# The last eight input blocks of a down-projection: from plain products to seven products per output pair

## The chip, the cores and the metric

The kernel runs on one core of one Trainium2 chip. The metric is the device time of one execution in microseconds (us), lower is better. [...]

## The reference

One layer of a decoder on 1024 tokens of width 1024, in float32: a norm, two attentions, gates, a residual, then a norm and a gated MLP of width 2816 with a short convolution, a residual, and a last norm. The part that matters here:

```python
def conv_ffn(xn, w_up, conv_w, conv_b, w_down):
    u = xn @ w_up
    ...
    gate, val = jnp.split(c, 2, axis=-1)
    return (jax.nn.silu(gate) * val) @ w_down      # (1024 x 2816) @ (2816 x 1024)

x = x + conv_ffn(xn, ...)
return rmsnorm(x, norm_final_w)
```

## The kernel before

All matrices are cut in blocks of 128 by 128; activations lie transposed, so that a tile holds 128 features by 1024 tokens, used as two halves of 512. TensorE multiplies in a reduced float format, so each float32 operand is split into a high part (a cast on ScalarE) and a low part (source minus high, on VectorE). A product of two blocks is then three matmuls: high by high, high by low, low by high. `split` and `parts_h` make the two parts of an activation, `load_w` and `split_pair` those of weights.

The down-projection (`down`) has 22 input blocks (the hidden tiles `hd`, which the earlier part stored in DRAM) and 8 output blocks, and it works in three stages.

*Blocks 0 to 5* are multiplied plainly, in 16 pieces (three blocks and one output each, both halves).

*Blocks 6 to 13* go by a seven-product scheme. The output pair m and m + 4, the two token halves, and two groups of four input blocks make a 2 by 2 by 2 product of large blocks. With A the weights (A11, A12 for output m; A21, A22 for m + 4) and B the activations, seven products of large blocks do in place of eight: A11 B11, A12 B21, S1 T1, S2 T2, S3 T3, S4 B22 and A22 T4. The S are sums of weight blocks, made on GpSimd by `sum_pair`; the T are differences of the activation blocks, made on VectorE by `sums_h`, once for all outputs. A product is 4 blocks by 3 matmuls. For each of the four pairs the kernel first makes A11 B11 (kept in a bank `y`) and A12 B21, and then, in a second loop over the pairs, the five others. Every product is added from its bank into `x3`, the residual stream, by VectorE.

*Blocks 14 to 21* are again multiplied plainly. Their activations come in by `load_h` in the second loop, four for each pair (`late`). Then follow, for each half of the tokens, all eight outputs, 24 matmuls each; the weights are loaded twice, once for each half. The last two outputs of the second half go in quarters of 256 tokens. `evac` adds the bank into `x3`, squares on ScalarE, adds the squares up, and multiplies by the last norm's weight.

`last_norm` gives the closing steps of a half or a quarter as a list: column sums of the squares on TensorE, the power on GpSimd, the spreading over partitions on TensorE, and the scales with their output transfers. These are taken out one by one between the products of later outputs.

Weights are fetched one step ahead: `next_w` takes the next entry of a queue and `ahead` prepares the one after it. The pool `wp` has three `raw` tiles for loads and two each of `wh` and `wl`; `uw` has two each of `sh` and `sl` for split sums; the sums themselves lie in two tiles `c`. Activation parts lie in 28 slots (`hp` with 19 and `hpb` with 9), used in turn; loads go through nine tiles `hr`. A scheduler orders each engine's instructions by the order in the code and by when it reckons their operands ready; at run time each engine keeps that order.

Of the kernel before, what the change touches and what calls it, by code (L numbers as in the profile page):

```python
# [17 lines left out]
P = 128  # L18
D = 1024
T = 1024  # L20
KC = D // P
# [8 lines left out]
DEFER = (4,8)  # L30
N1 = 6
LPAD, RPAD = 288, 480
HOLD = 1
# [10 lines left out]
class Trunk:  # L44
# [24 lines left out]
    def ahead(self, n):  # L69
        while len(self.wq) < n and self.wsrc and (self.wsrc[0][1] != "pair" or self.uw):  # L70
            src, nk, *eng = self.wsrc.pop(0)
            if nk == "sums":

                self.sums = self.split_pair(*self.sum_pair(src, True, "sl"), 1, 3)
            elif nk == "rest":
                self.sums["A22"] = self.load_w(src[1][:, 4:8], 4)
                self.wq.append(self.sums)
            elif nk == "pair":
# [28 lines left out]
    def split_pair(self, g, v, sa, sb, skip=0, end=4):  # L107
# [3 lines left out]
        for pool, h, l, src, names in ((self.wp, "wh", "wl", g, ("A11", "A12")), (self.uw, "sh", "sl", sa, ("S1", "S2")),  # L111
# [16 lines left out]
            for i, name in enumerate(names):  # L128
                ops[name] = hi[:, i], lo[:, i]
        self.pin, self.after = False, None  # L130
        return ops

# [73 lines left out]
    def run(self):  # L206
        nc, tc = self.nc, self.tc
        with ExitStack() as ctx:
# [20 lines left out]
            self.x2d = self.dp.tile([8, P, T], F32, name="x2d")  # L229
            self.hd = self.dp.tile([NF, P, T], F32, name="hd")  # L230
            self.yd = self.dp.tile([8, P, T], F32, name="yd")
            self.wp = ctx.enter_context(tc.tile_pool(name="wp", bufs=2))
# [14 lines left out]
    def plan(self):  # L247
# [20 lines left out]

        n, n2 = N1 // 2, NF - N1 - 8
        self.pieces = [(m, c) for m0 in (4, 0) for c in range(2) for m in range(m0, m0 + 4)]  # L270
# [600 lines left out]

    def product(self, ps, a, b, ks=range(4), first=True, last=True, skip=False, low_last=False):

# [3 lines left out]
        if low_last:  # L877
            for n, k in enumerate(ks):
                for i, x in enumerate(self.B[b, k]):
                    nc.tensor.matmul(ps, ah[:, k, :], x, start=first and n == i == 0, stop=False, skip_group_check=skip)  # L880
            for n, k in enumerate(ks):
                i = nc.tensor.matmul(ps, al[:, k, :], self.B[b, k][0], start=False, stop=last and n == len(ks) - 1, skip_group_check=skip)
            return i
        for n, k in enumerate(ks):
            bh, bl = self.B[b, k]
            nc.tensor.matmul(ps, ah[:, k, :], bh, start=first and n == 0, stop=False, skip_group_check=skip)  # L886
# [104 lines left out]
    def open_down(self):  # L991
        tc = self.tc
        self.dctx = ExitStack()
        self.hrp = self.dctx.enter_context(tc.tile_pool(name="hrp", bufs=HR, reuse_waits="tile"))
        self.hp = self.dctx.enter_context(tc.tile_pool(name="hp", bufs=HP, reuse_waits="tile"))
        self.nh = 0
# [5 lines left out]

    def parts_h(self, src):

        h = self.tl(self.hp if self.nh % (HP + HPB) < HP else self.hpb, [P, 2, H2], "h", F32R)
        self.nh += 1
        return self.split(h[:, 0], h[:, 1], src)
# [62 lines left out]
    def down(self):  # L1070

        nc, tc = self.nc, self.tc
        with ExitStack() as ctx:
# [3 lines left out]
            self.uw = e(tc.tile_pool(name="uwd", bufs=2, side="right", reuse_waits="tile"))  # L1077
            self.hpb = e(tc.tile_pool(name="hpb", bufs=HPB, side="right", reuse_waits="tile"))
            self.sfp = self.cpl, "c"
# [18 lines left out]
            def one(name, k, j, hf):  # L1098
                self.B[name, k] = self.parts_h(self.raw_h(N1 + j, hf))

            preps += [lambda k=k, n=n, o=o, hf=hf: one(n, k, k + o, hf) for n, o, hf in (("B11", 0, 0), ("B21", 4, 0), ("B22", 4, 1)) for k in range(4)]
            sums = [lambda k=k: self.sums_h(k) for k in range(4)]
# [37 lines left out]
            for m in range(4):  # L1140
# [30 lines left out]
            acc = self.tl(self.uw, [P, 2, H2], "sh")  # L1171
            js = range(N1 + 8, NF)
            q = H2 // 2

            def evac(ps, m, hf, a=0, b=H2):

                x = x3[:, m, hf * H2 + a:hf * H2 + b]
                tt(x, x, ps, ALU.add)
                sum_ = acc[:, hf, a:b]
                sq = sum_ if m == 0 else self.tl(self.uw, [P, b - a], "sl")  # L1180
                nc.scalar.activation(sq, x, AF.Square)
                if m and (m < KC - 1 or not hf):
                    tt(sum_, sum_, sq, ALU.add)
                nc.scalar.mul(x, x, self.vecs[:, C_NO + m:C_NO + m + 1])
                return sq

            tail = []
            for hf in range(2):
                for m in range(KC if hf == 0 else KC - 2):
                    w = self.next_w()  # L1190
                    ps = bank(m % 2)
                    mms(ps, w, hf, js)
                    evac(ps, m, hf)
                    for _ in range(1 if m < 4 else len(tail)):
                        if tail:
                            tail.pop(0)()
                if hf == 0:
                    tail = self.last_norm(psD, [acc[:, 0]], x3, 0, 0, H2, ((0, 2, nc.vector), (6, 8, nc.gpsimd), (2, 4, nc.vector), (4, 6, nc.vector)))

            ws = [(m, self.next_w()) for m in (KC - 2, KC - 1)]  # L1200
            for a, b in ((0, q), (q, H2)):
                for m, w in ws:
                    ps = bank(m % 2)[:, :q]
                    mms(ps, w, 1, js, a, b, lambda n, m=m: tail.pop(0)() if a and n == (4 if m < KC - 1 else 2) else None)
                    sq = evac(ps, m, 1, a, b)
                tail = self.last_norm(psD, [acc[:, 1, a:b], sq], x3, H2, a, b, ((0, 1, nc.vector), (1, 3, nc.vector), (6, 8, nc.gpsimd), (3, 6, nc.vector)) if a else
                                      ((0, 3, nc.gpsimd), (3, 5, nc.vector), (5, 8, nc.vector)))
# [98 lines left out]
```

## Time and profile before

| | |
|---|---|
| median of 3 runs | 1348.9 us (1347.94 to 1349.32) |
| the profiled execution | 1349.12 us |
| its span, first to last instruction | 1347.3 us |
| mean granted TensorE clock | 0.997 |
| five-product loop of blocks 6 to 13 | 1192.5 to 1246.9 us |
| last eight blocks | 1246.9 to 1337.8 us |
| closing norm and output after the last product | 1337.8 to 1347.3 us |

In the lines of windows, the first two numbers are the stretch and its length; then follow the busy time of PE, PEld (weight loads), DVE, ACT and POOL with the number of instructions in brackets, the granted clock, the share of the DMA engines and GB/s. In lists by time, a line has the start, the duration, engine, source line and operation, and in brackets how long the engine was idle before it and what released it.

### The profile page before, as it was taken

How to read it: one execution, taken by the hardware profiler on the slowest of the kernel's cores; microseconds unless marked ns; L12 is line 12 of the kernel's file. 1: busy time of each engine (PE TensorE's matmuls, PEld its weight loads, DVE VectorE, ACT ScalarE, POOL GpSimd, SP SyncE). 2: the span in 40 equal slices, each digit the busy share in tenths (PEclk: the TensorE clock that was granted, in tenths of full speed). 3: DMA queues.
4: the chain of work that ended last, by engine and by line, in shares of the span. 5: the costliest groups of instructions: out<-in, count | busy, mean ns of one | idle time of the engine just before them, and what ended most of it. 6: DMA issues, size and time to landing. Idle time of an engine off the chain costs nothing.

```text
span 1347.3 us, 17300 instructions
## 1 busy us (share of the span) xinstructions
PE 1328.9 (99%) x6304; PEld 1104.6 (82%) x6304; DVE 1036.0 (77%) x1557; ACT 616.1 (46%) x1003; POOL 470.6 (35%) x349
## 2 busy tenths in 40 slices
PE   7999999999999999999999999999999999999997
PEld 6888888888888777878888888888888888888887
DVE  7847775289899875465678999999999987986454
ACT  8432232276667665333454444444444434433343
POOL 0336552000102124641455555565555511231011
PEclk9999999999999999999999999999999999999998
DMA  6423443866553235334433222222222238552342
GB/s 257 146 105 150 148 156 141 251 175 188 141 149 130 87 114 207 129 110 155 141 107 96 79 79 94 78 94 74 83 94 74 86 136 315 197 180 67 94 138 81
DMA packets 62468, 179.48 MB, mean 133 GB/s; under 512 B 6832, under 2 KB 15152, under 8 KB 62384
## 3 DMA queue, kind: packets, MB, share of 16 engines
q1 hardware_dynamic: 50928, 160.98, 36.9%
q10 hardware_dynamic: 11456, 17.41, 3.5%
q8 instruction: 49, 0.80, 0.2%
q14 instruction: 35, 0.29, 0.1%
HBM read 129.61 MB, written 48.76 MB: 132 GB/s over the span
## 4 chain that ended last, share of the span: by engine, by line
PE 88%; POOL 4%; DVE 3%; DMA 3%; ACT 1%; issue 1%; POOLq 0%; SPq 0%; ACTq 0%; DVEq 0%
PE t L886 13%; PE t L887 13%; PE t L888 13%; PE y L1091 3%; PE d L1091 3%; PE t L880 3%; PE g L180 3%; PE sc L602 3%; PE g L181 3%; PE g L182 3%; PE y L1118 2%; PE d L1118 2%; DMA gr<-gd 2%; PE sc L182 2%; PE sc L181 2%; PE sc L180 2%
## 5 line engine op out<-in xcount | busy, mean ns | idle before, releaser
L1049 ACT ACTIVATE c<-us,vecs 128x512 f32<-128x512 f32 x80 | 61.3, 780 | 132.5 <-POOL us L1043 128.5
L1051 DVE SCALAR_TENSOR_TENSOR c<-us,vecs,c 128x512 f32<-128x512 f32 x160 | 110.4, 748 | 8.6 <-ACT c L1049 8.6
L145 ACT CAST wh<-raw 128x1024 fp32r<-128x1024 f32 (+2 forms) x60 | 60.8, 1013 | 107.6 <-PE sc L181 30.5
L1043 POOL TENSOR_TENSOR us<-us,rstd 128x1024 f32<-128x1024 f32 x38 | 99.6, 2641 | 4.5 <-DVE us L435 2.4
L147 DVE TENSOR_TENSOR wl<-raw,wh 128x1024 fp32r<-128x1024 f32 (+2 forms) x60 | 75.0, 1250 | 33.3 <-ACT wh L145 21.8
L123 DVE TENSOR_TENSOR sl<-sf,sh 128x1024 fp32r<-128x1024 f32 x62 | 87.5, 1413 | 11.5 <-ACT sh L122 11.5
L122 ACT CAST sh<-sf 128x1024 fp32r<-128x1024 f32 x62 | 63.4, 1048 | 60.4 <-PE t L887 44.2
L123 DVE TENSOR_TENSOR wl<-raw,wh 128x1024 fp32r<-128x1024 f32 (+1 forms) x35 | 74.2, 2120 | 3.7 <-ACT wh L122 3.6
L98 POOL TENSOR_TENSOR sf<-rv 128x512 f32<-128x512 f32 x30 | 41.2, 1375 | 100.6 <-DVE sl L123 57.9
L180 PE MATMUL g<-xh,wh 128*128 128x512 f32 x176 | 70.6, 401 | 0.1
L182 PE MATMUL g<-xh,wl 128*128 128x512 f32 x176 | 70.3, 400 | 0.0
L181 PE MATMUL g<-xl,wh 128*128 128x512 f32 x176 | 70.3, 399 | 0.0
L197 POOL TENSOR_TENSOR rs<-ms,mhalf 128x8 f32<-128x8 f32 (+2 forms) x9 | 14.5, 1607 | 157.7 <-DVE ms L195 147.1
L103 POOL TENSOR_TENSOR sf<-raw,rv 128x512 f32<-128x512 f32 x30 | 40.7, 1356 | 65.4 <-DVE sl L123 65.4
L606 DVE CUSTOM_DVE_ANT_0 L<-sc,bias 128x128 f32<-128x128 f32 (+7 forms) x64 | 47.7, 751 | 17.0 <-PE sc L602 13.9
L585 POOL MEMSET aT<- 128x128 f32 x32 | 6.1, 204 | 151.6 <-PE t L631 101.3
L607 ACT ACTIVATE L<-L,sm 128x128 f32<-128x128 f32 (+7 forms) x64 | 49.6, 778 | 20.0 <-DVE sm L606 17.3
L760 POOL TENSOR_TENSOR gr<-gr,rstd 128x1024 f32<-128x1024 f32 x16 | 41.2, 2583 | 41.7 <-DMA gr<-gd 41.5
L123 DVE TENSOR_TENSOR wl<-rv,wh 128x512 fp32r<-128x512 f32 x30 | 49.3, 1642 | 3.5 <-ACT wh L122 3.5
L1053 ACT ACTIVATE c<-c 128x512 f32<-128x512 f32 x40 | 24.0, 600 | 60.8 <-DVE c L1051 60.8
L602 PE MATMUL sc<-u,u 128*128 128x512 f32 (+2 forms) x192 | 49.6, 358 | 0.0
L182 PE MATMUL sc<-mh,wl 128*128 128x512 f32 x126 | 49.1, 390 | 0.3 <-DVE wl L147 0.3
(515 smaller groups left out, 4334.7 us busy)
## 6 DMA issues: line engine op xcount, KB each, us to landing
u<-qd SPq DMA_DIRECT2D x72, 256.0 KB, 6.5
raw<-in_w_down SPq DMA_DIRECT2D x27, 512.0 KB, 3.6
raw<-in_w_in SPq DMA_DIRECT2D x25, 512.0 KB, 4.2
hr<-hd SPq DMA_DIRECT2D x50, 256.0 KB, 5.4
raw<-in_w_up SPq DMA_DIRECT2D x23, 512.0 KB, 3.5
hd<-c SPq DMA_DIRECT2D x22, 512.0 KB, 2.6
rv<-in_w_up SPq DMA_DIRECT2D x21, 512.0 KB, 3.5
gr<-gd SPq DMA_DIRECT2D x16, 512.0 KB, 3.6
```

Of the source, the lines that this page charges most:

```text
L123: j = nc.vector.tensor_tensor(lo, src, hi.bitcast(F32), ALU.subtract)
L147: self.lo = (eng or nc.vector).tensor_tensor(wl, raw, wh.bitcast(F32), ALU.subtract)
L180: nc.tensor.matmul(ps, wh[:, kc + o, :], ah, start=first and n == 0, stop=False)
L181: nc.tensor.matmul(ps, wh[:, kc + o, :], al, start=False, stop=False)
L182: nc.tensor.matmul(ps, wl[:, kc + o, :], ah, start=False, stop=last and n == len(kcs) - 1)
L602: nc.tensor.matmul(sc[:, lo + n0:lo + n1], qs, k[c][part][:, n0:n1], start=part == 0, stop=part == 1)
L886: nc.tensor.matmul(ps, ah[:, k, :], bh, start=first and n == 0, stop=False, skip_group_check=skip)
L887: nc.tensor.matmul(ps, ah[:, k, :], bl, start=False, stop=False, skip_group_check=skip)
L888: i = nc.tensor.matmul(ps, al[:, k, :], bh, start=False, stop=last and n == len(ks) - 1, skip_group_check=skip)
L1043: (nc.vector if j == 0 else nc.gpsimd).tensor_tensor(u[:, 2:], u[:, 2:], self.rstd, ALU.mult)
L1051: nc.vector.scalar_tensor_tensor(c, u[:, o + k:o + k + H2], col(m, k), c, ALU.mult, ALU.add)
L1091: nc.tensor.matmul(ps, v[:, n, :], x, start=n == i == 0, stop=n == len(js) - 1 and i == 2)
```

## The change

The last eight blocks use seven products too. Even and odd blocks (14, 16, 18, 20 and 15, 17, 19, 21) form the two groups. `second_pair` loads a pair's two weight tiles, makes four sums on GpSimd, splits A11, A12, S2, S3 and A22 and stores the sums S1 and S4 in DRAM (`sd`). Five products of each pair run in a loop: A11 B11, A12 B21, the previous pair's S3 T3, A22 T4, S2 T2. The last two, S1 T1 and S4 B22, follow for all pairs at the end, in one bank one after the other, with their weights loaded from `sd`; pairs 2 and 3 do them in quarters. Weights are loaded once, and their sums written and read once more.

The activations come in twice. Eight raw loads (512 KB each) go into the slots that B11 and B21 of blocks 6 to 13 leave; there `diffs` makes the four differences in place, behind chosen adds of the pairs m = 0, 1 and 2. B11, B21 and B22 are loaded again through `hr`. Their splits go into named slots (`old` finds those of the former T tiles): B11, B21, T4, T2 and T3 are traced before the new loop (`prepare(24)`), T1 and B22 within it. The sums of squares lie in four `hr` tiles (`box`).

```diff
+    def second_pair(self, src, m):
...
+        tt(sa[:, 0], v[:, 0], v[:, 1], ALU.add)
+        tt(sb[:, 0], sa[:, 0], g[:, 0], ALU.subtract)
+        tt(sb[:, 1], g[:, 0], v[:, 0], ALU.subtract)
+        tt(sa[:, 1], g[:, 1], sb[:, 0], ALU.subtract)
+        nc.sync.dma_start(self.sd[m], sa.rearrange("p a k c -> p (a k) c"))
+        ops = {}
+        for pool, h, l, x, names in ((self.wp, "wh", "wl", g, ("A11", "A12")), (self.uw, "sh", "sl", sb, ("S2", "S3")), (self.wp, "wh", "wl", v[:, 1:2], ("A22",))):
...
-        src += [(self.w_dn[m, :, N1 + 8:, :], n2) for _ in range(2) for m in range(KC)]
+        src += [((self.w_dn[m, :, N2:, :], self.w_dn[m + 4, :, N2:, :]), "second", m) for m in range(4)]
+        src += [(self.sd[m], 8) if m < 2 else (self.sd[m], "idle") for m in range(4)]
...
-            late = [(hf, j) for hf in range(2) for j in range(N1 + 8, NF)]
+            old = lambda n, k: (base + 12 + 4 * k + "T1 T2 T3 T4".split().index(n)) % (HP + HPB)
...
+            def diffs(k, after):
+                b11, b12, b21, b22 = raws[k]
+                with tc.issue_after(after.ins):
+                    tt(b11, b12, b11, ALU.subtract)
+                    tt(b12, b22, b12, ALU.subtract)
+                    tt(b22, b22, b11, ALU.subtract)
+                    tt(b21, b22, b21, ALU.subtract)
...
+            more = [lambda k=k: read("B11", k, 0, 0, old("T1", k)) for k in range(4)]
+            more += [lambda k=k: read("B21", k, 1, 0, old("T2", k)) for k in range(4)]
+            more += [lambda k=k: ready("T4", k, base + 8 + k) for k in range(4)]
+            more += [lambda k=k: ready("T2", k, old("T4", k)) for k in range(4)]
+            more += [lambda k=k: ready("T3", k, old("T3", k)) for k in range(4)]
+            more += [lambda: box.append(self.tl(self.hrp, [P, H2], "hr")) for _ in range(4)]
+            more += [lambda k=k: ready("T1", k, base + 2 * k + 1) for k in range(4)]
+            more += [lambda k=k: read("B22", k, 1, 1, base + 2 * k) for k in range(4)]
...
+            for k in range(4):
+                load(k)
             for m, y in enumerate(ys):
...
-                tt(col(m + 4, 0), col(m + 4, 0), ps, ALU.subtract)
+                i = tt(col(m + 4, 0), col(m + 4, 0), ps, ALU.subtract)
+                if m in (1, 2):
+                    diffs(2 * m - 1, i)
                 self.product(y, w["S3"], "T3", first=False, skip=True)
                 for hf in range(2):
-                    tt(col(m + 4, hf), col(m + 4, hf), y, ALU.add)
-                for _ in range(4):
-                    hf, j = late.pop(0)
-                    self.load_h(j, hf)
...
+                    i = tt(col(m + 4, hf), col(m + 4, hf), y, ALU.add)
+                if m < 2:
+                    diffs(2 * m, i)
+            prepare(24)
...
+            def seventh(m):
+                self.product(ys[m], ws[m]["S3"], "2T3", first=False, skip=True)
+                evac(ys[m], m + 4, 0)
+                tt(col(m + 4, 1), col(m + 4, 1), ys[m], ALU.add)
+
+            for m in range(4):
+                w = self.next_w()
...
+                self.product(y, w["A11"], "2B11", skip=True, low_last=True)
+                tt(col(m, 0), col(m, 0), y, ALU.add)
+                self.product(ps, w["A12"], "2B21")
+                evac(ps, m, 0)
+                if m:
+                    seventh(m - 1)
+                ps = bank(0)
+                self.product(ps, w["A22"], "2T4")
+                tt(col(m + 4, 0), col(m + 4, 0), ps, ALU.subtract)
+                self.product(y, w["S2"], "2T2", first=False, skip=True)
+                tt(col(m, 1), col(m, 1), y, ALU.add)
+                prepare(4)
+            seventh(3)
...
+            def fifth(m, w, a=0, b=H2):
+                ps = bank(0)[:, :b - a]
+                self.product(ps, [x[:, 0:4] for x in w], "2T1", skip=True, cols=slice(a, b))
+                evac(ps, m + 4, 1, a, b)
+                return ps
+
+            def third(m, w, ps, a=0, b=H2, last=False):
+                self.product(ps, [x[:, 4:8] for x in w], "2B22", first=False, skip=True, cols=slice(a, b))
+                return evac(ps, m, 1, a, b, last)
```

More of the change, by code (lines that the diff above doesn't have):

```diff
@@ L31 @@
 N1 = 6
+N2 = N1 + 8
 LPAD, RPAD = 288, 480
@@ L870, in operands, with product @@
         tt(t4, t2, b21, ALU.subtract)
-    def product(self, ps, a, b, ks=range(4), first=True, last=True, skip=False, low_last=False):
+    def product(self, ps, a, b, ks=range(4), first=True, last=True, skip=False, low_last=False, cols=slice(0, H2)):
         nc = self.nc
@@ L879, in product @@
                 for i, x in enumerate(self.B[b, k]):
-                    nc.tensor.matmul(ps, ah[:, k, :], x, start=first and n == i == 0, stop=False, skip_group_check=skip)
+                    nc.tensor.matmul(ps, ah[:, k, :], x[:, cols], start=first and n == i == 0, stop=False, skip_group_check=skip)
             for n, k in enumerate(ks):
-                i = nc.tensor.matmul(ps, al[:, k, :], self.B[b, k][0], start=False, stop=last and n == len(ks) - 1, skip_group_check=skip)
+                i = nc.tensor.matmul(ps, al[:, k, :], self.B[b, k][0][:, cols], start=False, stop=last and n == len(ks) - 1, skip_group_check=skip)
             return i
         for n, k in enumerate(ks):
-            bh, bl = self.B[b, k]
+            bh, bl = (x[:, cols] for x in self.B[b, k])
             nc.tensor.matmul(ps, ah[:, k, :], bh, start=first and n == 0, stop=False, skip_group_check=skip)
@@ L1181, in evac @@
                 nc.scalar.activation(sq, x, AF.Square)
-                if m and (m < KC - 1 or not hf):
+                if hf in seen and not last:
                     tt(sum_, sum_, sq, ALU.add)
+                seen.append(hf)
                 nc.scalar.mul(x, x, self.vecs[:, C_NO + m:C_NO + m + 1])
                 return sq
[L1187 to L1198, printed above, removed]
@@ L1200, in down @@
-            ws = [(m, self.next_w()) for m in (KC - 2, KC - 1)]
-            for a, b in ((0, q), (q, H2)):
[L1202 to L1206, printed above, removed]
+            ys, ws = [], []
@@ new lines, in down @@
+            seventh(3)
+            assert not more
+            tail = self.last_norm(psD, [box[0]], x3, 0, 0, H2, ((0, 2, nc.vector), (6, 8, nc.gpsimd), (2, 4, nc.vector), (4, 6, nc.vector)))
+            def fifth(m, w, a=0, b=H2):
[6 more added lines that the diff above has]
+                return evac(ps, m, 1, a, b, last)
@@ new lines, in step @@
+            def step(n=1):
+                for _ in range(n):
+                    tail.pop(0)()
+            ws = [self.next_w() for _ in range(2)]
+            p = []
+            for m in range(2):
+                p.append(fifth(m, ws[m]))
+            step()
+            for m in range(2):
+                third(m, ws[m], p[m])
+                step()
+            ws += [self.next_w() for _ in range(2)]
+            for a, b in ((0, q), (q, H2)):
+                p = []
+                for m in (2, 3):
+                    p.append(fifth(m, ws[m], a, b))
+                    step()
+                sqs = [box[1][:, a:b], third(2, ws[2], p[0], a, b, True)]
+                if not a:
+                    step()
+                sqs.append(third(3, ws[3], p[1], a, b, True))
+                assert not tail
+                tail = self.last_norm(psD, sqs, x3, H2, a, b, ((0, 1, nc.vector), (1, 3, nc.vector), (6, 8, nc.gpsimd), (3, 6, nc.vector)) if a else
```

63 lines of the change are left out of this document (52 added, 11 removed).

## The prediction

> **What bounds the kernel now.** I read the page's busy line first, then the windows by stage, then the chain, and last VectorE's and GpSimd's own lists in time. The windows are cut at the stage borders: the MLP's hidden part, the four output pairs of the first seven-product part (m = 0 to 3), the start of the last eight blocks, the end.
>
> ```profile
> PE 1328.9 (99%) x6304; PEld 1104.6 (82%) x6304; DVE 1036.0 (77%) x1557; ACT 616.1 (46%) x1003; POOL 470.6 (35%) x349
> core 0: us, PE busy (x) PEld busy (x) DVE busy (x) ACT busy (x) POOL busy (x), PEclk, DMA share, GB/s
> 720.00:1100.00 380.00, 380.00 (x1678) 314.67 (x1677) 364.22 (x430) 166.00 (x227) 201.17 (x155) 1.00 0.25 84
> 1192.50:1206.10 13.60, 13.60 (x62) 11.26 (x61) 12.56 (x16) 3.24 (x6) 6.23 (x5) 1.00 0.65 210
> 1206.10:1219.70 13.60, 13.60 (x62) 11.26 (x61) 7.60 (x10) 2.74 (x4) 5.22 (x5) 1.00 0.25 80
> 1219.70:1233.30 13.60, 13.60 (x62) 11.26 (x61) 8.22 (x10) 3.16 (x4) 2.54 (x2) 1.00 0.26 79
> 1233.30:1246.90 13.60, 13.60 (x62) 11.26 (x61) 11.84 (x17) 6.85 (x10) 0.00 (x0) 1.00 0.14 39
> 1246.90:1268.70 21.80, 21.80 (x98) 18.06 (x97) 8.23 (x10) 7.11 (x10) 0.00 (x0) 1.00 0.33 98
> 1324.90:1337.80 12.90, 12.90 (x111) 12.90 (x109) 6.30 (x11) 5.34 (x10) 2.01 (x2) 1.00 0.03 10
> 1337.80:1347.30 9.50, 2.06 (x12) 1.49 (x11) 2.46 (x5) 1.30 (x3) 2.50 (x3) 0.61 0.59 208
> ```
>
> TensorE fills every stage of the down-projection at full clock; nothing holds it until 1337.8, and 9.5 us of closing norm and output follow. So a matmul taken out is worth its whole spacing as long as VectorE (DVE) keeps up. DVE has spare time there: 7.60 and 8.22 of 13.6 us busy in m = 1 and 2, 8.23 of 21.8 in the last part.
>
> ```profile
> 1246.94 5.44 PE d L1091 x24
> 1252.38 5.44 PE y L1091 x24
> 1319.53 5.44 PE y L1091 x24
> 1324.97 2.87 PE d L1091 x24
> ```
>
> In the chain, one output half of the last eight blocks is 24 matmuls in 5.44 us: 0.2267 us for one of 512 columns, and 2.87 / 24 = 0.120 for one of 256.
>
> **What goes.** Before, the last blocks take 16 output halves of 24 matmuls, 384 in units of 512 columns (the last two outputs' second halves run as quarters of 256). After, they take 4 pairs x 7 products x 12 = 336, with as many quarters as before (2 pairs x 2 products x 2 quarters x 12 = 96). So 48 go: 48 x 0.2267 = **10.88 us**. The 28 products of 2.72 us last 76.2 us instead of 87.1. [...]
>
> **What DVE gains.** Prices first; the lists give start, duration, engine, line.
>
> ```profile
> 1169.35 0.68 DVE L1018 TENSOR_TENSOR hr<-hr,hr 128x512 f32<-128x512 f32 x1
> 1169.95 0.68 DVE L1016 TENSOR_TENSOR hr<-hr,hr 128x512 f32<-128x512 f32 x1
> 1234.58 1.22 DVE L123 TENSOR_TENSOR sl<-c,sh 128x1024 fp32r<-128x1024 f32 x1
> 1235.71 0.68 DVE L800 TENSOR_TENSOR h<-hr,h 128x512 fp32r<-128x512 f32 x1
> ```
>
> Start to start, a 512-wide operation costs 0.60 us and a 1024-wide one 1.13. Added are 16 in-place differences (9.6 us), 12 more operand splits (28 for 16: 7.2) and 16 more PSUM adds into x3 (9.6); the weight splits stay about even: (1.13 + 1.13 + 0.60) x 4 and 4 x 1.13 make 16.0 us, against 16 x 1.13 = 18.1. That is some 24 us more DVE work in a stretch about 11 us shorter. Three places matter.
>
> *m = 1 and 2 of the first part.* The differences are put behind chosen adds there: two sets of four in m = 1 (one just past m = 0's last add), two around m = 2, 4.8 us each. DVE goes from 7.60 to 12.4 and from 8.22 to 13.0 of 13.6. Nothing is late by itself: the adds have four banks to hide in. Their eight raw loads (4 MB) wait on SP for B11's and B21's slots, which TensorE's first products release by 1192.5; the pair loads queue behind them. The DMA share is 0.65 and then 0.25, so they land within m = 0 and 1, before their differences. I put both at nothing; without that cover DVE would stand at a difference for about one landing, the 3.6 us of this row:
>
> ```profile
> raw<-in_w_down SPq DMA_DIRECT2D x27, 512.0 KB, 3.6
> ```
>
> *The entry to the new part.* New operands go into the slots of old ones, so they can be split only as the last pair (m = 3: five products of 12 x 0.2267 = 2.72 us from 1233.3) releases those: B11 into T1's at 1236.0, B21 into T2's at 1238.8, T4 into B22's at 1241.5, T2 into T4's at 1244.2, T3 into T3's at 1246.9. They are wanted at 1246.9, 1249.7, 1252.4, 1255.1, and for T3 at 1263.3. The product S2 T2 also accumulates into bank y, so it waits for the add that reads A11 B11 out of it, and that add was traced behind T3's splits. DVE's list from 1233.3 to that add: 10 adds (6.0), S34 of m = 3, A11 and S2/S3 of the new pair (3 x 1.13 = 3.4), its A22 (0.6), 20 splits (12.0): **22.0 us**, for 21.8 until S2 T2 is due at 1255.1. Undisturbed it just fits. It isn't undisturbed:
>
> ```profile
> 1189.58 1.30 POOL L98 TENSOR_TENSOR c<-raw 128x512 f32<-128x512 f32 x1 [24.83 <-DMA raw<-in_w_down]
> 1190.84 1.75 POOL L103 TENSOR_TENSOR c<-raw,raw 128x512 f32<-128x512 f32 x1
> 1192.56 1.74 POOL L102 TENSOR_TENSOR c<-c,raw 128x512 f32<-128x512 f32 x1
> 1194.37 1.62 POOL L104 TENSOR_TENSOR c<-raw,c 128x512 f32<-128x512 f32 x1
> 1191.36 0.68 DVE L1147 TENSOR_TENSOR x<-x,y 128x512 f32<-128x512 f32 x1
> 1191.95 4.59 DVE L800 TENSOR_TENSOR h<-hr,h 128x512 fp32r<-128x512 f32 x3
> 1222.27 1.29 POOL L103 TENSOR_TENSOR c<-raw,raw 128x512 f32<-128x512 f32 x1 [5.74 <-DVE sl L123]
> ```
>
> While GpSimd (POOL) forms a pair's weight sums, three splits took 4.59 us (1.53 each), while the add from PSUM kept its 0.68. Those three cost 4.59 - 1.80 = 2.8 us. POOL's own operation grew from 1.30 to about 1.7. The new pair 0's sums wait for the tile c that S34 of m = 3 gives back (1234.58 + 1.22 = 1235.8), as the last row's waited; pair 1's follow some 8 us later. So POOL runs through much of exactly this stretch, and it makes 0 to 2 x 2.8 = 5.6 us more. With pair 1's A11 split possibly ahead (1.13) and the differences of m = 1 and 2 slowed in the same way (POOL ran 5.22 and 2.54 us there; at 2.8 per 5.1 us that is 2.9 and 1.4, against room of 1.2 and 0.6, so 2.5 carried over), TensorE stands between 0 and 0.2 + 5.6 + 1.1 + 2.5 = 9.4 us. I take **4 us**: most of one pair's disturbance and part of the other's, as the splits are about half of DVE's list and the row's 2.8 is for splits alone. The next thing late would be pair 1's A11 remainder, which its product uses last and which has 1.8 us of cover.
>
> *The loop and the tail.* A pair from m = 1 on costs DVE 8 adds (4.8), 2.9 of weights, 2.4 of T1 or B22 splits and 2.8 of disturbance: 12.9 of 13.6 us. The bank y now has 8.2 us of cover instead of 5.4, so I count nothing; at the far end 1 us a pair. The stored sums (512 KB out and in for each pair) follow 13.6 us apart, and SP's next weight loads queue behind a store that waits for POOL; each landing is 3 to 4 us, hidden unless that store slips by more than 5. In the tail, bank d is shared by S1 T1 and S4 B22, so the second waits until the first is read: 2.72 us of cover in whole halves, 1.43 in quarters, where a scale of 1.21 us may be ahead on DVE.
>
> ```profile
> 1302.93 1.21 DVE L1238 TENSOR_TENSOR x<-x,d 128x1024 f32<-128x1024 f32 x1
> 1332.50 0.36 PE L188 MATMUL d<-ones,sl 128*128 128x1 f32 x2
> 1332.72 0.36 PE L188 MATMUL d<-ones,sh 128*128 128x1 f32 x2
> ```
>
> Each quarter's column sums read three tiles instead of two: 2 more matmuls of one column at 0.22 / 2 = 0.11 us, twice: 0.44, of which the last quarter hides one. I count **0.3 us**; the waits in the quarters are between 0 and 4 x 0.4 = 1.6, and I take 0, since the last adds are dropped there. The closing 9.5 us stay.
>
> **Sum.** The profiled execution took 1349.12 us with a span of 1347.3, 0.2 us above the median of the runs shown, 1348.9. 1349.1 - 10.9 + 0.3 + 4.0 = 1342.5, and against the median **1342.3 us**, 0.5% faster. About 0.2% (2.7 us) is what a measurement can tell from no change: 1346.2 to 1351.6.
>
> **The rivals.**
>
> *DVE keeps up.* For it: in the hidden part DVE is 364 of 380 us busy with POOL at 201, and TensorE never waits. Against it: there operands stand ready for the next block, here slots open one by one. No stall gives 1348.9 - 10.9 + 0.3 = 1338.3. Chance 0.20.
>
> *The gain is eaten.* Both disturbances in full, the carried lateness too, and the loop's 1 us: 8 to 11 us of stalls, 1346.3 to 1349.3. Chance 0.14.
>
> *Slower: entry splits one by one behind POOL.* DVE serves its list in order; if pair 0's and pair 1's sums run without a gap while the 16 splits of B11, B21, T4 and T2 are made, each costs 1.53 instead of 0.60, 14.9 us in all, with TensorE standing at each product for its own four. That gives 1348.9 - 10.9 + 0.3 + 14.9 = 1353.2; it decides from 13.3 us of stalls. For it: POOL's 1.7 us each when disturbed, eight sums, 13.7 us. Against it: that covers only about half of the stretch, and adds from PSUM pass undisturbed. Chance 0.14.
>
> *The clock falls in the stall.*
>
> ```profile
> 1338.00:1340.00 2.00, 0.83 (x6) 0.74 (x6) 0.41 (x2) 0.92 (x2) 0.47 (x2) 0.99 0.46 160
> 1340.00:1342.00 2.00, 1.12 (x4) 0.72 (x4) 0.66 (x2) 0.23 (x1) 0.56 (x1) 0.50 0.75 265
> ```
>
> Within the last 4 us, where TensorE is busy 1.95 of 4, the granted clock goes from 0.99 to 0.50. [...] Against it: the lateness shows as several waits (B21, T4, T2, y) with matmuls between. Chance 0.08.
>
> **How the numbers follow.** The forecast, 2 to 7 us of stalls (1340.3 to 1345.3), has 0.44. Faster by over 0.2%: 0.44 + 0.20 + 0.08 = 0.72; within: 0.14; slower: 0.14. The range runs from just under the forecast's end into the case of no stall, 1338.8 (which leaves its lower part out), to the end of the eaten gain, 1349.0; the slower case lies outside.
>
> **What would show it.** The page's TensorE count falls by 48 and rises by 4, to 6260. In the windows TensorE stays full up to about 1246.9; then the waits should list TensorE behind DVE's splits and the add on y within the first four products, some 4 us in all, with splits of about 1.5 us while POOL is busy and 0.68 otherwise. The loop from pair 1 on should hold 13.6 us per pair with DVE over 90%. I am wrong in kind if TensorE waits for a DMA or ScalarE there, if it loses several us per pair in the loop or in the quarters, or if the differences hold up m = 1 and 2.

## The result and the profile after

The changed kernel takes 1343.6 us (median of 7 executions, 1343.26 to 1346.88), the kernel before 1348.68 beside it (7 executions, 1347.94 to 1349.32): a ratio of 0.9968, 95% interval 0.9956 to 0.9979. Run again in a later comparison it took 1343.65 against 1348.13, 0.9965 (0.9953 to 0.9978). So it is faster by 0.3%, 4.5 to 5.1 us, where 10.9 us of matmuls were taken out and 6.6 us were forecast.

The busy line and windows of the kernel after, at the same stages as the prediction's (all stages come 2.3 us earlier, because an earlier part of this execution was shorter by that). PE is TensorE, DVE VectorE, ACT ScalarE, POOL GpSimd, SP the queue of SyncE that issues most of the transfers; PSUM are the accumulator banks.

```profile
PE 1321.7 (99%) x6264; PEld 1097.4 (82%) x6264; DVE 1065.8 (79%) x1603; ACT 621.7 (46%) x1019; POOL 495.6 (37%) x365
```

```profile
1203.80:1217.40 13.60, 13.60 (x62) 11.14 (x61) 13.42 (x16) 3.21 (x5) 6.67 (x5) 1.00 0.23 77
1217.40:1231.00 13.60, 13.53 (x60) 10.89 (x59) 13.46 (x19) 3.10 (x3) 5.00 (x3) 1.00 0.27 79
1231.00:1244.60 13.60, 13.60 (x62) 11.27 (x61) 13.60 (x20) 12.55 (x22) 5.78 (x4) 1.00 0.23 77
1244.60:1262.06 17.46, 15.14 (x58) 11.19 (x57) 17.46 (x23) 5.88 (x10) 5.67 (x4) 0.90 0.29 93
1262.06:1275.66 13.60, 13.60 (x61) 11.26 (x60) 11.62 (x16) 6.43 (x9) 7.80 (x4) 1.00 0.44 134
1275.66:1289.26 13.60, 13.60 (x61) 11.26 (x60) 11.93 (x14) 7.71 (x11) 6.33 (x4) 1.00 0.47 173
```

Before, VectorE had 7.60 and 8.22 of 13.6 us to do in m = 1 and 2. Now it is full from there to the end of the entry (13.42, 13.46, 13.60, 17.46 of 17.46), and the entry is the one stage in which TensorE stands: 2.3 of 17.46 us. From pair 1 on TensorE is full again. The granted clock of the entry, 0.90, is the second thing to see.

How TensorE's wait at the entry comes about is read from the list by time, GpSimd first, then VectorE, ScalarE and TensorE:

```profile
1243.94 1.30 POOL L148 TENSOR_TENSOR c<-raw 128x512 f32<-128x512 f32 x1 [4.83 <-DMA raw<-in_w_down]
1245.20 1.74 POOL L150 TENSOR_TENSOR c<-raw,raw 128x512 f32<-128x512 f32 x1
...
1244.32 1.47 DVE L158 TENSOR_TENSOR wl<-raw,wh 128x512 fp32r<-128x512 f32 x1
1245.71 3.47 DVE L832 TENSOR_TENSOR h<-hr,h 128x512 fp32r<-128x512 f32 x2
...
1250.30 7.30 DVE L832 TENSOR_TENSOR h<-h,h 128x512 fp32r<-128x512 f32 x12
1257.53 1.21 DVE L158 TENSOR_TENSOR wl<-raw,wh 128x1024 fp32r<-128x1024 f32 x1
...
1248.67 1.05 ACT L157 CAST sh<-c 128x1024 fp32r<-128x1024 f32 x1 [3.50 <-POOL c L149]
...
1253.48 1.22 ACT L831 CAST h<-h 128x512 fp32r<-128x512 f32 x2 [3.23 <-DVE h L832]
1254.61 1.04 ACT L157 CAST wh<-raw 128x1024 fp32r<-128x1024 f32 x1
...
1255.70 2.52 PE L912 MATMUL y<-h,wh 128*128 128x512 f32 x8 [1.86 <-ACT wh L157]
```

While GpSimd makes the sums of pair 1, a low part of 512 columns takes VectorE 1.47 us, and two splits 3.47, instead of 0.60 each. So the twelve splits of T4, T2 and T3 begin late. ScalarE's casts of T1 (1253.48) may only write the slots that the splits of T4 and T2 have read, so they wait 3.23 us for VectorE, and behind them in ScalarE's queue stands its cast of pair 1's A11 (1254.61). The schedule has put the product with that A11 ahead of pair 0's S2 T2. TensorE waits for it; its wait list names the last link only:

```profile
PE y L912 <- ACT wh L157: 1.9, 1, 1.9
PE d L919 <- DVE h L832: 0.3, 1, 0.3
```

The second loss stands in windows of 1 us, where the last three columns are the granted clock, the DMA share and GB/s:

```profile
1256.00:1257.00 1.00, 1.00 (x6) 0.77 (x5) 1.00 (x3) 1.00 (x3) 0.00 (x0) 1.00 0.00 0
1257.00:1258.00 1.00, 1.00 (x4) 0.79 (x3) 1.00 (x3) 0.21 (x1) 0.00 (x0) 0.62 0.00 0
1258.00:1259.00 1.00, 0.85 (x3) 0.20 (x2) 1.00 (x2) 0.00 (x0) 0.00 (x0) 0.50 0.00 0
1259.00:1260.00 1.00, 1.00 (x3) 0.81 (x4) 1.00 (x2) 0.00 (x0) 0.00 (x0) 0.50 0.26 37
1260.00:1261.00 1.00, 1.00 (x5) 0.76 (x4) 1.00 (x3) 0.00 (x0) 0.00 (x0) 0.67 0.73 221
```

After the gap the clock is 0.50 for some 3.4 us (1257.24 to 1260.66 by these windows) and TensorE, though busy, does half: 0.38 + 0.50 + 0.50 + 0.33 = 1.7 us lost. In the list by time this looks like further waits (four matmuls in 2.03 us, where the last four ahead of the gap took 1.07); only windows this fine tell the two apart. Where the expectations below speak of 5.0 us of stalls at the entry, 1.7 of them were this.

At the end, the column sums of the last quarter, before and after, from TensorE's list:

```profile
1338.76 0.38 PE L188 MATMUL d<-ones,sl 128*128 128x1 f32 x2 [0.84 <-ACT sl L1181]
1339.00 0.36 PE L188 MATMUL d<-ones,sh 128*128 128x1 f32 x2
1339.22 0.36 PE L188 MATMUL d<-ones,sl 128*128 128x1 f32 x2
```

```profile
1330.29 0.35 PE L218 MATMUL d<-ones,hr 128*128 128x1 f32 x2
1330.97 0.38 PE L218 MATMUL d<-ones,hr 128*128 128x1 f32 x2 [0.33 <-ACT hr L1261]
1331.82 1.43 PE L218 MATMUL d<-ones,hr 128*128 128x1 f32 x8 [0.46 <-ACT hr L1261]
1334.28 0.69 PE L233 MATMUL d<-ident,rs 128*128 128x128 f32 x2 [1.03 <-POOL rs L227]
```

Three operands, the sum so far and two squares, come one behind the other now, where there were two, and eight records stand behind the last of them instead of six. The clock plays a part here too: it falls in the end of every profile, in this one at 1332.3, under these eight records. Where it fell later (after_again), the same eight took 1.05 us instead of 1.43.

### The profile page after: what moved, and what is told of

It is laid out like the page before. It is cut to its first block, busy times and chain, and to the rows that moved or that the text cites. A ratio compares the mean times of both kernels' runs of the same rounds, so it can differ in the third digit from the quotient of the medians.

```text
span 1341.1 us, 17306 instructions
## 1 busy us (share of the span) xinstructions
PE 1321.7 (99%) x6264; PEld 1097.4 (82%) x6264; DVE 1065.8 (79%) x1603; ACT 621.7 (46%) x1019; POOL 495.6 (37%) x365
## 4 chain that ended last, share of the span: by engine, by line
PE 86%; DVE 5%; POOL 4%; DMA 2%; issue 2%; ACT 1%; POOLq 0%; SPq 0%; ACTq 0%; DVEq 0%
PE t L920 13%; PE t L919 13%; PE t L918 13%; PE g L210 3%; PE g L211 3%; PE g L212 3%; PE t L912 3%; PE sc L634 3%; PE y L1157 2%; PE d L1157 2%; PE sc L212 2%; PE sc L210 2%; PE sc L211 2%; DMA gr<-gd 2%; PE d L918 2%
## 5 line engine op out<-in xcount | busy, mean ns | idle before, releaser
L177 DVE TENSOR_TENSOR wl<-raw,wh 128x1024 fp32r<-128x1024 f32 (+2 forms) x46 | 57.7, 1255 | 30.2 <-ACT wh L175 18.9
L175 ACT CAST wh<-raw 128x1024 fp32r<-128x1024 f32 (+2 forms) x46 | 46.0, 1001 | 62.6 <-PE sc L211 30.5
L227 POOL TENSOR_TENSOR rs<-ms,mhalf 128x8 f32<-128x8 f32 (+2 forms) x9 | 13.6, 1517 | 96.5 <-DVE ms L225 85.9
```

## The experiments

All profiles are cut the same way: "projection" runs from the down-projection's first matmul to the first matmul of the quarters, "end" from there to the last instruction; "half clock" is half the time that the clock stood at 0.50 within the projection, by the windows of 1 us. That is about what TensorE lost to it, except in sums_later: there 3.0 of the 6.8 us lie in its longest wait, so that about 1.9 were lost. The expectations' "stretch" is projection and end together, with a start read 0.2 us later in the kernel after (237.9 for 238.1). Ratios are to the kernel before in the same comparison.

| kernel | median, us | ratio (95%) | projection | half clock | end |
|---|---|---|---|---|---|
| before | 1347.4 to 1348.7 | 1 | 219.5 | 0 | 22.5 |
| after | 1343.60 | 0.9968 (0.9956 to 0.9979) | 213.9 | 1.7 | 24.2 |
| after_again | 1343.65 | 0.9965 (0.9953 to 0.9978) | 213.0 | 0 | 23.4 |
| old_operands | 1337.71 | 0.9930 (0.9915 to 0.9945) | 208.8 | 0 | 23.8 |
| two_pairs_no_sums | 1338.61 | 0.9940 (0.9925 to 0.9954) | 211.2 | 0 | 23.7 |
| sums_unread | 1342.77 | 0.9960 (0.9945 to 0.9975) | 213.8 | 1.7 | 24.2 |
| t3_after_add | 1343.26 | 0.9969 (0.9958 to 0.9981) | 215.4 | 1.7 | 23.4 |
| t1_b22_later | 1343.81 | 0.9973 (0.9963 to 0.9983) | 212.9 | 0 | 23.8 |
| both_orders | 1344.12 | 0.9973 (0.9962 to 0.9983) | 215.7 | 3.4 | 23.8 |
| orders_sums_later | 1338.68 | 0.9935 (0.9916 to 0.9954) | 210.1 | 0 | 24.2 |
| sums_later | 1347.88 | 0.9999 (0.9990 to 1.0008) | 217.7 | 3.4 | 23.9 |
| closing | 1343.42 | 0.9966 (0.9954 to 0.9978) | 215.3 | 0 | 22.9 |
| all_three | 1339.16 | 0.9929 (0.9916 to 0.9943) | 210.1 | 0 | 23.0 |

The theories: VectorE is late at the entry because GpSimd's sums slow it (A in the later expectations); or the operands are made in an order in which one late instruction holds up others that were ready (B).

**old_operands.** The new products read the first part's operands; no new activation work is made (`load`, `diffs` and the 28 splits are left out).

```diff
             def diffs(k, after):
+                return
...
-            for k in range(4):
-                load(k)
...
-            prepare(24)
...
+            for (n, k), x in list(self.B.items()):
+                self.B["2" + n, k] = x
```

> All activation work of the last eight blocks is left out (eight raw loads, 16 differences, 28 splits and their loads); its products read the operands of blocks 6 to 13, so the output is another. TensorE's list is unchanged. If what is missing of the 10.9 us is VectorE's and ScalarE's work at the entry, the gaps there go to 0 and the stretch to the end falls from 237.9 to about 232.9, 5 us faster than the changed kernel; if part of it is in the loop or in matmuls that run slower, it stays above 234.

The projection took 208.8 us, 10.7 less than before, with no wait listed in it. So the term of the matmuls, 10.88 us, is right, and whatever is missing from it comes through the new activation work.

**two_pairs_no_sums** and **sums_unread.** In the first, pairs 0 and 1 of the new part take raw weights for all four sums and GpSimd makes none for them. In the second, GpSimd makes the sums again, but nobody reads them.

```diff
...
         tt(sa[:, 1], g[:, 1], sb[:, 0], ALU.subtract)      # with the three above it left out in the first, m < 2
...
+        if m < 2:
+            sb = g
```

> GpSimd's sums of pairs 0 and 1 of the last eight blocks are left out: the loaded weights take their place, so the output is another. If the sharing between GpSimd and VectorE makes the stall (its splits and differences of 1.19 to 1.74 us for 0.60 in this stretch add up to some 4 us), all those fall to 0.68 and the gaps go from 5.0 to 1 or less. If the order alone makes it, with VectorE's list as long as it is, the sum stays at 4 or more.

> GpSimd still makes the four sums of pairs 0 and 1 of the last eight blocks, but nobody reads them: the splits of S2 and S3 and the store of these two pairs take the raw weights instead (so the S2, S3, S1 and S4 products of pairs 0 and 1 have wrong operands). It differs from two_pairs_no_sums (stretch from the first down-projection matmul to the end 234.8 us, no stall at the entry) only in that GpSimd works beside VectorE again, while ScalarE still waits for none of its results. Theory A (GpSimd's sums stretch VectorE's two-operand work, VectorE's list is what is late): the stall returns, 3 to 5 us at pair 1's A11, stretch 237 to 239. Theory B (the lateness is ScalarE's cast of S2 and S3 standing in its queue for GpSimd's result, 3.50 us at 1248.67, and what it holds up behind it): the stall stays below 1 us, stretch 235.

Without the sums no wait was left at the entry; the projection was 211.2 us, and the two waits that were listed lie elsewhere (0.9 and 0.4 us, ending at 1216.7 and 1277.6). With sums that nobody reads the wait was back, with the very figures of the kernel after. First two rows of VectorE without the sums, then VectorE and ScalarE with unread sums:

```profile
1245.53 0.68 DVE L163 TENSOR_TENSOR wl<-raw,wh 128x512 fp32r<-128x512 f32 x1
1246.13 1.28 DVE L837 TENSOR_TENSOR h<-hr,h 128x512 fp32r<-128x512 f32 x2
```

```profile
1246.48 3.48 DVE L834 TENSOR_TENSOR h<-hr,h 128x512 fp32r<-128x512 f32 x2
...
1245.73 1.04 ACT L159 CAST sh<-raw 128x1024 fp32r<-128x1024 f32 x1
...
1254.25 1.22 ACT L833 CAST h<-h 128x512 fp32r<-128x512 f32 x2 [6.96 <-DVE h L834]
1255.38 1.04 ACT L159 CAST wh<-raw 128x1024 fp32r<-128x1024 f32 x1
```

The cast of the sums (1245.73) waits for nothing now, and still the casts of T1 wait 6.96 us for VectorE and the cast of A11 comes as late. So ScalarE's 3.50 us at GpSimd's result, which I had taken for a rival cause, cost nothing here; that GpSimd's work beside VectorE is what makes VectorE late is shown. The same two splits take 3.48 us beside the sums and 1.28 without them; what the two engines take from each other, no trace shows.

**t3_after_add**, **t1_b22_later**, **both_orders.** Orders alone: T3's splits behind pair 0's first addition; T1's and B22's a pair later; both.

```diff
-            prepare(24)
+            prepare(16)                            # t3_after_add, both_orders
...
+                if m == 0:
+                    with tc.issue_after(i.ins):    # i: the add of A11 B11 into x3
+                        prepare(4)
...
-                prepare(4)                         # end of the loop's body
+                if m in (1, 2):                    # t1_b22_later, both_orders
+                    prepare(4)
```

> T3's four splits are traced behind pair 0's add of A11 B11 instead of ahead of it; nothing else moves. Measure: the gaps between matmuls from 1244.9 to 1266 in the changed kernel (5.0 us in all), and the time from the down-projection's first matmul to the end (241.8 us before, 237.9 changed). If VectorE's order makes the stall (the add stands behind 12 splits and three weight splits), the add comes 2 to 3 us earlier and the gaps fall from 5.0 to about 2.5. If ScalarE's order makes it (pair 1's A11 cast stands behind two T1 casts that wait for VectorE), the 2.0 us gap at pair 1's A11 stays and the sum is 4.5 or more.

> The splits of T1 and B22 are traced one pair later, and their casts are ordered behind pair 1's and pair 2's closing ScalarE operations. If ScalarE's order makes the stall, pair 1's A11 cast no longer waits 3.2 us and the 2.0 us gap goes: 5.0 to 3 us or less. If VectorE's order makes it, the add of A11 B11 stays as late as it is (1260.4 on the changed kernel's scale), TensorE loses the same time a product later, and the sum stays at 4 to 5.

> The two changes of order in one kernel, nothing left out: T3's four splits are made behind pair 0's first addition instead of ahead of the loop, and the splits of T1 and B22 one pair later. Each alone left one half of the entry's stall: with the first, pair 1's A11 waits 1.8 us for ScalarE's cast (stretch 238.7 us), with the second 2.9 us for VectorE's low part (stretch 236.5). Theory B (order of the queues alone): with both, neither engine is late, stalls at the entry under 1.5 us, stretch 234 to 235.5. Theory A (VectorE has too much to do up to there because GpSimd slows it): VectorE is ahead by four splits of 0.60 us, so the stall is 2.9 less 2.4, under 1 us too, but VectorE's rows beside GpSimd's sums are still 3.47 us for two splits. What tells them apart is what ends the wait that is left: ScalarE's cast (B) or VectorE's low part (A). Neither holds if the stall stays above 3 us.

None differs from the kernel after by more than the intervals (0.9969, 0.9973, 0.9973 against 0.9968). The wait only changed its name: in the first it is still ScalarE's cast, since the casts of T1 never waited for T3's splits; in the second it is VectorE's low part of the same A11. The longest of each:

```profile
PE y L912 <- ACT wh L157: 1.8, 1, 1.8
```

```profile
PE y L914 <- DVE wl L158: 2.9, 1, 2.9
```

```profile
PE y L918 <- DVE x L1281: 2.9, 1, 2.9
```

My expectation for both_orders, under 1.5 us, was wrong: with only six matmuls of pair 1's A11 product left in between, TensorE came to S2 T2 of pair 0, and the add that frees bank y stood on VectorE behind two low parts of pair 1's weights:

```profile
1255.81 1.21 DVE L158 TENSOR_TENSOR wl<-raw,wh 128x1024 fp32r<-128x1024 f32 x1
1256.94 1.21 DVE L158 TENSOR_TENSOR sl<-c,sh 128x1024 fp32r<-128x1024 f32 x1
1258.08 0.68 DVE L1281 TENSOR_TENSOR x<-x,y 128x512 f32<-128x512 f32 x1
```

This is the wait that the prediction had named.

**orders_sums_later** and **sums_later.** GpSimd's sums of pair 1, and the splits of S2 and S3 from them, are moved behind splits of the entry: with both orders, or alone.

```diff
+            i = tt(sa[:, 0], v[:, 0], v[:, 1], ALU.add)
+            if m == 1:
+                self.tc.add_manual_dep(i.ins, self.lo.ins.name, ...)   # self.lo: the split made last
...
+                    self.made()                    # these sums and their split, in the loop at m = 0
```

> As both_orders, and GpSimd's sums of pair 1, with the splits of S2 and S3 from them, wait for T2's last split: they run from about 1255 us instead of from 1243.94, beside the loop and not beside the entry's splits. Nothing is left out. Theory A: the 20 splits of the entry lose their stretch (two of them took 3.47 us instead of 1.3), stalls at the entry 0 to 0.5 us, stretch 233 to 234. Theory B (order alone): no gain over both_orders. Risk for both: the sums now stretch VectorE in the loop, where it is busy over nine tenths; if it has no room there, a stall of 1 to 2 us appears at pair 1's S2 product or later, and the stretch is 235 or more.

> Only the place of GpSimd's sums of pair 1 is changed: with the splits of S2 and S3 made from them they wait for T2's last split; the splits of T3, T1 and B22 stay where the change has them. Nothing is left out. Theory A (what makes the entry late is VectorE slowed beside these sums): two splits at 1245.71 take 1.28 us instead of 3.47 and the low part of A22 0.68 instead of 1.47, so VectorE is 3.0 us earlier, ScalarE's casts of T1, which wait for its splits, too, and of the entry's 5.0 us 0 to 2 are left; stretch 233 to 235. Theory B (the order of T1's casts and T3's splits ahead of pair 1's A11 is the cause): the wait for ScalarE's cast of A11 stays near 1.9 us whatever GpSimd does, 4 to 5 us at the entry, stretch 237 to 238. Between them (2 to 4 us left): both are needed, as in orders_sums_later, which left 0.7.

As built, the sums of the first wait for T3's last split, not T2's as its expectation says; those of the second for T2's. The first gave nearly what A expects (projection and end 234.3 us, for 233 to 234): 1338.68 us, 5.4 less than both_orders beside it. GpSimd, then VectorE:

```profile
1257.23 1.29 POOL L159 TENSOR_TENSOR c<-raw 128x512 f32<-128x512 f32 x1 [17.98 <-DVE h L845]
...
1245.06 1.28 DVE L845 TENSOR_TENSOR h<-hr,h 128x512 fp32r<-128x512 f32 x2
...
1247.46 4.90 DVE L845 TENSOR_TENSOR h<-h,h 128x512 fp32r<-128x512 f32 x8
...
1253.41 0.68 DVE L1294 TENSOR_TENSOR x<-x,y 128x512 f32<-128x512 f32 x1
```

The two splits take 1.28 us, the add of bank y comes at 1253.41, and of the waits 0.6 us is left. The second went against both theories: no gain, 4.2 us slower than the kernel after beside it. GpSimd, ScalarE, VectorE, and TensorE's longest wait:

```profile
1253.78 4.55 POOL L159 TENSOR_TENSOR c<-raw 128x512 f32<-128x512 f32 x1 [13.24 <-DVE h L845]
...
1260.81 1.04 ACT L151 CAST sh<-c 128x1024 fp32r<-128x1024 f32 x1 [5.67 <-POOL c L162]
...
1248.74 7.31 DVE L845 TENSOR_TENSOR h<-h,h 128x512 fp32r<-128x512 f32 x12
...
1262.41 0.69 DVE L152 TENSOR_TENSOR wl<-raw,wh 128x512 fp32r<-128x512 f32 x1 [5.22 <-ACT wh L151]
1263.02 0.68 DVE L1296 TENSOR_TENSOR x<-x,y 128x512 f32<-128x512 f32 x1
...
PE y L931 <- DVE x L1296: 5.1, 1, 5.1
```

Here VectorE's twelve splits kept their pace (7.31 us), and GpSimd's first sum lost: 4.55 us instead of 1.29. The cast of the sums stood on ScalarE ahead of A22's cast, A22's low part on VectorE ahead of the add of bank y, and TensorE waited 5.1 us for that add. So both theories hold a half: the sums must not run beside the splits, and the instructions that wait for them must not stand ahead of what TensorE wants next. Moving one alone gains nothing; moved together they gain 4 to 5 us.

**closing.** The end alone.

```diff
-        for b in range(n):
-            for k, sq in enumerate(sqs):
+        for k, sq in enumerate(sqs):               # the last quarter's column sums only
+            for b in range(n):
...
-                sqs = [box[1][:, a:b], third(2, ws[2], p[0], a, b, True)]
+                sq = third(2, ws[2], p[0], a, b, a > 0)
+                sqs = [box[1][:, a:b], sq][:2 if a else 1]
```

> Only the end is changed, nothing left out: the square of output block 2 in the last but one quarter is added on VectorE again, so that its column sums take 8 records of TensorE instead of 12; in the last quarter the column sums go operand by operand, so that only the last square's own two stand behind it; and ScalarE scales block 2 after both squares instead of between them. If the closing is longer for these three reasons: 0.44 us for four records of 0.11, 0.44 for four records behind the gate, 0.42 for ScalarE's scaling of 0.51 between the squares: 1.3 us, stretch 236.6 instead of 237.9. Rival: the gate is VectorE's additions behind the scaling of the third quarter (1330.06 us); then only the first 0.44 and part of the second are saved, stretch 237.3.

The end was 22.9 us, against 23.4 to 24.2 in the ten profiles with the end unchanged. These ten differ by where the clock falls in the end: 24.2 us where it falls up to 15.7 us behind the quarters' first matmul, 23.4 where it falls 17.9 us or more behind it, the others between. In this profile it falls between the column sums and the spreading, as in old_operands, t1_b22_later and both_orders, which have 23.8 us: like beside like, the closing gains 0.9 us, not the 1.3 expected. The rows of TensorE that answer to those above:

```profile
1332.08 1.29 PE L225 MATMUL d<-ones,hr 128*128 128x1 f32 x8
1333.62 0.61 PE L225 MATMUL d<-ones,hr 128*128 128x1 f32 x4 [0.24 <-ACT hr L1268]
```

Four records instead of eight stand behind the gate, and the quarters take 12.71 us instead of 13.16. The time does not show it (0.9966 against 0.9968): this profile's projection, whose order is that of the kernel after, took 215.3 us. In this run the first matmul of each of the two columns sets the start flag, while the sums of both are open in one bank, and the output is another (relative error 0.357). The number and kind of instructions are the same, so its time is read as meant. In all_three only the very first matmul sets the flag, and no such error is left.

**all_three** and **after_again.** orders_sums_later with this closing; the changed kernel once more.

> orders_sums_later with the closing of the run closing; the last quarter's column sums set the bank's start flag only on their first matmul, so that no operand is lost. Nothing is left out. If the two gains lie in different places they add: 4.0 us at the entry (0.7 of 5.0 left) and 1.2 at the end (from the last quarter's first matmul to the end 22.9 us instead of 24.15): stretch 234.2 less 1.2, 233.0; span about 1336, time about 1337.5, 0.8% below the kernel before. If the closing's start depends on how VectorE leaves the loop, less of the 1.2 appears.

> The changed kernel, unaltered, beside the two others on the same chip. Both theories: as before, time 1343.6 us, the wait at pair 1's A11 near 2 us for ScalarE's cast, stretch 237.9. A stretch more than 0.5 us from that says how much one profiled execution's stretch can be trusted.

all_three has the lowest ratio of those that leave nothing out: 0.9929 of the kernel before, 4.5 us under the changed kernel beside it. Against orders_sums_later (0.9935) its closing is seen only in the profile (23.0 us for 24.2, of which some is the clock's fall, 16.3 us behind the quarters' first matmul for 15.7). after_again has the same wait of 1.9 us, and no fall of the clock:

```profile
1257.00:1258.00 1.00, 0.52 (x3) 0.09 (x1) 1.00 (x2) 0.00 (x0) 0.00 (x0) 1.00 0.00 0
1258.00:1259.00 1.00, 0.73 (x3) 0.65 (x4) 1.00 (x2) 0.00 (x0) 0.00 (x0) 1.00 0.00 0
```

## Why the prediction came out as it did

The forecast was 1342.3 us, faster by 0.5%; it was faster by 0.3 to 0.35%, inside the range. Step by step:

- *48 matmuls, 10.88 us*: right; 10.7 in old_operands.
- *m = 1 and 2, nothing late by itself*: right, with VectorE fuller than counted (13.42 and 13.46 of 13.6 us, for 12.4 and 13.0). In two runs a wait of 0.9 us appeared there.
- *The entry, 4 us, of 0 to 9.4*: the size was good and the source too, VectorE's list stretched by GpSimd's sums (3.47 us for two splits, where 1.53 each was the price taken). In the two profiles of the changed kernel the projection gained 5.6 and 6.4 us of 10.9, so 5.3 and 4.4 were lost, 1.7 of the 5.3 to the clock. That the size came out is in part luck: the forecast added VectorE's lateness up to the add of bank y, the rows show 3.0 us of it (2.2 in the two splits, 0.8 in the low part), and TensorE lost its time at another operand. What failed is where it would show. I wrote that I would be wrong in kind if TensorE waited for ScalarE there, and it did, 1.9 us, for pair 1's A11, because the schedule put that product ahead of S2 T2. I had followed VectorE's list and not the casts of T1 that wait on it ahead of A11's on ScalarE. The prediction did name pair 1's A11, as the next thing late, but its remainder, the low part from VectorE; what was late first was its high part, ScalarE's cast. (In after_again the low part follows, 0.7 us.)
- *The loop, 13.6 us a pair*: right, without loss. VectorE's share was 85 to 88% in pairs 1 and 2, not over 90.
- *Column sums, 0.3 us, and the closing unchanged*: too small. The end took 0.9 us more in one profile and 1.7 in the other. Each extra matmul of one column is two records, so TensorE's count is 6264 and not 6260, and the price is 0.22 us, not 0.11: the quarters take 13.16 us for 12.70. The rest is the third operand in the chain of the last quarter, and the place of the clock's last fall: where that is as in the kernel before, between the column sums and the spreading, the end is 1.3 us longer (23.8 for 22.5, in old_operands, t1_b22_later and both_orders); in the first profile it came earlier, in the second later.
- *The clock falls in the stall*, chance 0.08: it happened in the first profile of the changed kernel, and in all in five of the eight in which one listed wait was 1.8 us or more. My reason against it, that the lateness would be several short waits, was wrong. What a fall inside the projection costs, no run had shown; it was 1.7 us, half of the 3.4 us at 0.50. The end of the trace before was a weaker likeness than I took it for: in the 3.41 us ahead of its fall (1336.55 to 1339.96) TensorE was busy 2.19, in as long a time ahead of the fall at the entry (1253.83 to 1257.24) 1.55.
- *DVE keeps up*, 1338.3: its condition, splits undisturbed at the entry, is what orders_sums_later makes, and that took 1338.68. The figures are nearer than the cases: beside its own kernel before (1347.35) that is 8.7 us, where 10.6 were counted, and its end is 1.7 us longer. *The gain is eaten*, 1346.3 to 1349.3: not in the changed kernel; sums_later came to it. *Entry splits one by one behind POOL*, 1353.2: not seen; eight sums did not run without a gap (the first at 1227.32, three from 1233.98 to 1239.1, four from 1243.94 to 1250.3).

The sum by what was measured: 10.9 less 3.6 of waits at the entry and smaller ones, less 1.7 of clock, less 1.7 at the end is 3.9 us, the difference of the two profiles from the down-projection on; in after_again 10.9 less 4.4 less 0.9 is 5.6. The medians say 5.1 and 4.5.

What stays open: three profiles of one and the same order before the quarters (after, after_again, closing) gave projections of 213.0 to 215.3 us, 0 to 1.7 of which is clock. The rest is small waits in changing places that I did not follow, so differences of 2 us between single profiles are not read as effects above. Nor do the other executions say how often the clock falls at the entry: a mean clock of 0.997 stands for a profile with the fall (t3_after_add) and for profiles without it.

## What to carry to other kernels

When a product is taken out, follow the operands of its successors through every in-order queue that they pass: here the late engine (VectorE), the engine that TensorE was seen to wait for (ScalarE) and the cause (GpSimd) were three different ones, and moving any one link only moved the wait. In this kernel the sums on GpSimd belong where VectorE has no splits that TensorE waits for (two took 3.47 us beside the sums, 1.28 without), and what reads them belongs behind the work that is wanted next; the two had to be changed together. Cut the windows to 1 us around a gap before counting the time behind it as waiting.

## What the runs showed of the hardware that was not expected

- Behind gaps of about 2 us between matmuls the granted clock went from 1.00 to 0.50 in some profiles and not in others: with the same listed wait of 1.8 to 1.9 us it fell in after, sums_unread and t3_after_add, and not in after_again and closing; with the wait of 5.1 us (sums_later) and one of 2.9 (both_orders) it fell for twice as long, with the other of 2.9 (t1_b22_later) not at all. The clock stood at half in the projection for 3.4 us (after, sums_unread, t3_after_add) or 6.8 (both_orders, sums_later), and for nothing between. In the five profiles the 3.4 us ahead of the fall held 1.84 to 2.25 us without a matmul. In each of these traces the fall at the end comes 22 or 23 whole steps of 3.413 us after the first (in after at 1332.32 and 1257.24, 75.08 us or 22 such steps). Counted in the same steps from that last fall, the emptiest such stretch of the other three held 1.74 (after_again), 1.67 (closing) and 1.93 us (t1_b22_later). So idle time alone does not decide: 1.93 us passed without a fall, 1.84 did not, and at the end of the kernel after the 3.41 us ahead of the fall (1328.91 to 1332.32) held 0.80. What does decide was not shown.
- GpSimd's sums and VectorE's splits slow each other by turns or one alone: 3.47 us for two splits with 1.74 for a sum (after), or splits at 0.60 with 4.55 for a sum (sums_later). In the first case GpSimd's sum had begun (1243.94) beside an add from an accumulator bank, in the second (1253.78) amid twelve splits without a pause; whether that decides which loses was not tested.
